# Turning the second attention's softmax weights of heads 0 to 3 on VectorE and by on-chip transfers

## The chip, the cores and the metric

The kernel runs on one core of a Trainium2 chip. A core has TensorE (PE, with its weight loads as PEld), VectorE (DVE), ScalarE (ACT), GpSimd (POOL) and SyncE (SP, which here only issues transfers). The metric is the device time of one launch in microseconds (us); before the change the median of 3 runs is 832.18 us (831.88 to 832.41).

## The reference

Two layers of a hybrid decoder on 256 tokens of width 1024 in float32. Each layer normalises the rows, multiplies by one wide matrix, and feeds three token mixers whose gated outputs are added; then comes a squared-ReLU MLP. The second attention ("MoBA") has 8 heads of width 64. Its block is 256 tokens long, as long as the sequence, so no earlier block can be selected and what is left is plain causal attention per head:

```python
s_own = jnp.einsum('bhqd,bhkd->bhqk', qc, k_own).astype(jnp.float32) * scale
s_own = jnp.where(kpos[None, :] <= qpos[:, None], s_own, NEG_INF)
p = jax.nn.softmax(jnp.concatenate([s_sel, s_own], axis=-1), axis=-1).astype(v.dtype)
o_own = jnp.einsum('bhqk,bhkd->bhqd', p[..., topk * BS:], v_own)
```

The scores leave TensorE with queries on the partitions, and so does the softmax. The product with the values sums over keys, and so needs the weights with keys on the partitions: the matrix p of every head has to be transposed ("turned").

## The kernel before

Every weight matrix is streamed from HBM in blocks of 128 by 1024 float32 (`raw`, seven buffers, issued by SP, L195). Each block is split into a rounded part by ScalarE (`whi`, L210) and a remainder by VectorE (`wlo`, L212), six buffers each, and a product is three matmuls over these parts (`three`, L231 to L233; for matrices kept transposed L412 and L414). A list of units, `prog`, holds the projections in order; `at(slot, step)` hangs smaller steps behind a unit, and a scheduler then orders each engine's instructions from this program order. What `tc.keep_in_program_order` or `tc.manual_schedule` covers stays where it was written. A transfer signals one of eight completion semaphores, taken in turn over all queues. A transfer that takes a semaphore again waits until the transfer that had it eight earlier has landed.

The second attention runs beside the projections around it. Its first slot is the second block of the gate projection `gmoba1`. The units behind it are two more blocks of `gmoba1`, four of the branch matrix `bmla`, four of `rqk` (queries and keys of the retention mixer), four of `rv`, four of `rg`, then the branch matrix `bmoba`, which is the first to read the attention's output.

- Scores (`together`, L481): heads 0 to 3 in the first slot, heads 4 to 7 eight slots later (`GAP = 8`). Each head's scores are one PSUM bank of three 128 by 128 squares: queries 0 to 127 with keys 0 to 127, then queries 128 to 255 with all 256 keys.
- Softmax (`attention_head`): VectorE adds the mask and finds maxima (L495, L498), ScalarE takes exponentials (L504), VectorE divides (L507, L509). The result is the tile `prob`, 128 by 384, four buffers.
- Turn (L512 to L518): three TensorE transposes into a PSUM bank `ps_pt` (L515) and one ScalarE copy into `probT` (L517). Heads 0 to 3 are turned three and four slots behind their scores, heads 4 to 7 likewise.
- Values (L542, L544): in `rg`, behind the retention scores (`ps_r`), eight heads at 64 columns, with `probT` as the moving operand. `split_plain` (L252) then writes `omobah` and `omobal`.

Around the change run the two rotary steps of the retention queries and keys (`rope_turned`, L439). For each pair of column blocks SP issues four on-chip transfers that swap groups of 32 partitions (`qkoth`, L434), GpSimd multiplies (L446), and VectorE adds (L449). The tile `gn`, the group norm's gains and offsets, is loaded behind the first block of `rqk` and used behind `rg`.

Of the kernel before, what the change touches and what calls it, by code (L numbers as in the profile page):

```python
# [7 lines left out]
F32 = mybir.dt.float32  # L8
F32R = mybir.dt.float32r
BF16 = mybir.dt.bfloat16  # L10
AF = mybir.ActivationFunctionType
# [3 lines left out]
P = 128  # L15
D = 1024
S = 256
# [120 lines left out]
def trunk(ctx: ExitStack, tc: tile.TileContext, gx, wts, consts, gfin, gn, xtok, out):  # L138


    nc = tc.nc
    _, where, _ = weight_plan()
# [3 lines left out]
    sb = ctx.enter_context(tc.tile_pool(name="sb", bufs=1))  # L146
# [71 lines left out]
    def acc_tile(name="acc"):  # L218
        return ps.tile([P, 512], F32, name=name, tag="acc", bufs=4)

    def misc_tile(name="misc"):
        return ps.tile([P, 512], F32, name=name, tag="misc", bufs=4)

    def w2k(name):
        return sb.tile([P, 512], F32, name=name, tag="w2k", bufs=W2K)

    def t4(name):
        return sb.tile([P, 4, S], F32R, name=name, tag="t4", bufs=T4)

# [11 lines left out]
    def small(name):  # L241
        return sb.tile([P, 8], F32, name=name, tag="st", bufs=SMALL)
# [8 lines left out]
    def split_plain(src, hi, lo):  # L251
        return nc.scalar.activation(hi, src, AF.Copy), nc.vector.tensor_sub(lo, src, hi.bitcast(F32))  # L252
# [212 lines left out]
    def in_a_row(*jobs):  # L465


        with tc.manual_schedule(engines={mybir.EngineType.PE}):
            rest = [job() for job in jobs]
        for job in rest:  # L470
            job()

    def together(parts, heads):

        for banks, a, b in heads:
            for o, sa, sb_ in parts:
                for j, bank in enumerate(banks):
                    rows = slice(64 * j, 64 * j + 64)  # L480
                    nc.tensor.matmul(bank[:, o], a[rows, sa], b[rows, sb_], start=True, stop=True)  # L481

    def attention_head(score, scale):


        got = {}

        def scores(s_ps=None):
            if s_ps is None:
                s_ps = misc_tile("ps_s")  # L490
                score(s_ps[:, 0:P], slice(0, P), slice(0, P))
                score(s_ps[:, P : 3 * P], slice(P, S), slice(0, S))
            p = sb.tile([P, 3 * P], F32, name="prob", bufs=4)
            m = small("smx")
            nc.vector.tensor_tensor_reduce(  # L495
                p[:, 0:P], s_ps[:, 0:P], mask[:, P : 2 * P], 1.0, NEG_INF, ALU.add, ALU.max, m[:, 0:1]
            )
            nc.vector.tensor_tensor_reduce(  # L498
                p[:, P : 3 * P], s_ps[:, P : 3 * P], mask, 1.0, NEG_INF, ALU.add, ALU.max, m[:, 1:2]
            )  # L500
            nc.vector.tensor_scalar(m[:, 2:4], m[:, 0:2], -scale, None, op0=ALU.mult)  # L501
            spans = ((0, P), (P, 3 * P))
            for i, (a, b) in enumerate(spans):
                nc.scalar.activation(  # L504
                    p[:, a:b], p[:, a:b], AF.Exp, bias=m[:, 2 + i : 3 + i], scale=scale, accum_out=m[:, 4 + i : 5 + i]
                )
            nc.vector.reciprocal(m[:, 6:8], m[:, 4:6])  # L507
            for i, (a, b) in enumerate(spans):
                nc.vector.tensor_scalar(p[:, a:b], p[:, a:b], m[:, 6 + i : 7 + i], None, op0=ALU.mult)  # L509
            got["p"] = p  # L510

        def turn():  # L512
            pt = misc_tile("ps_pt")
            for i, src in enumerate((0, P, 2 * P)):
                nc.tensor.transpose(pt[:, P * i : P * i + P], got["p"][:, src : src + P], ident)  # L515
            pT = sb.tile([P, 3 * P], F32, name="probT", bufs=8)
            nc.scalar.activation(pT, pt[:, : 3 * P], AF.Copy)  # L517
            return pT  # L518

        return scores, turn  # L520

    def attention(oT, score, vs, scale, first, group=None, former=None):

        pT = {}

        def turned(h, turn):
            pT[h] = turn()

        def values(h0):


            o, v = acc_tile("po"), vs()
            for h in (h0 + 2, h0):
                cs = slice(S * (h - h0) // 2, S * (h - h0) // 2 + S)
                for i in range(2):
                    for j in (1, 0):
                        vh = v[i][:, VD * (h + j) : VD * (h + j) + VD]
                        dst = o[64 * j : 64 * j + 64, cs]  # L540
                        if i == 0:
                            nc.tensor.matmul(dst, vh, pT[h + j][:, 0:S], start=True, stop=False)  # L542
                        else:
                            nc.tensor.matmul(dst[:, P:S], vh, pT[h + j][:, S : 3 * P], start=False, stop=True)  # L544
            dst = (part[:, h0 // 2 : h0 // 2 + 2, :].rearrange("p k s -> p (k s)") for part in oT)
            return lambda: split_plain(o, *dst)


        blocks = [lambda: values(4), lambda: values(0)]
        heads = [attention_head(lambda o, qs, ks, h=h: score(h, o, qs, ks), scale) for h in range(8)]  # L550
        if group is None:
            for h, (scores, turn) in enumerate(heads):
                at(first + h, scores)
                at(first + h + 2, lambda h=h, turn=turn: turned(h, turn))
            return blocks

        def four(h0):
            banks = group(h0)

            def rest():  # L560
                for h, bank in enumerate(banks, h0):
                    heads[h][0](bank)

            return rest


        at(first, lambda: in_a_row(*former, lambda: four(0)))
        at(first + GAP, lambda: in_a_row(lambda: four(4)))
        for i in range(2):
            for h in range(4):  # L570
                at(first + GAP * i + 3 + h // 2, lambda h=4 * i + h: turned(h, heads[h][1]))
        return blocks[::-1]

    def gates(l, key, xn):
# [44 lines left out]
    def begin(key, tag=None, bufs=None, queue=nc.sync, parts=None):  # L619
        if tag:  # L620
            started[key] = sb.tile([P, 512 if tag == "w2k" else 1024], F32, name="raw0", tag=tag, bufs=bufs)
        else:
            started[key] = wp.tile([P, 1024], F32, name="raw", bufs=RAW)
        transfer(key, started[key], queue, parts)


    c = slice(G_END - 2 * KD, G_END + S)
# [6 lines left out]
    xrows = [w2k("xrow") for _ in range(2 * NT)]  # L634
    begin((0, "b0mq", 1), "t4", T4, parts=((0, 416), (416, 928)))
    for k in range(2, KD):
# [5 lines left out]
        if k < 5:  # L642
            begin((0, "b0mq", k), "t4", T4, parts=((0, 416), (416, 928)) if k == 2 else None)
        else:
# [18 lines left out]
    def at(slot, step):  # L663
        steps.setdefault(slot, []).append(step)

    def slot(key, j):
        return [k for k, _ in prog].index((key, j))
# [9 lines left out]
    def layer(l, xn, before):  # L677

        c0 = []
        c, mla, mqkv, rqkv = {}, {}, {}, {}  # L680
# [216 lines left out]
        first = slot("mv", 3)  # L897
# [23 lines left out]
        first = slot("gmoba1", 1)  # L921
        at(first, lambda: omobaT.extend((t4("omobah"), t4("omobal"))))

        def moba_scores(h0):
            banks = [misc_tile("ps_s") for _ in range(4)][::-1]
            together(
                ((slice(0, P), slice(0, P), slice(0, P)), (slice(P, 3 * P), slice(P, S), slice(0, S))),
                [(banks[2 * i : 2 * i + 2], *(qkT[key][h0 // 4][:, i, :] for key in ("mq", "mk"))) for i in range(2)],
            )
            return banks  # L930

# [19 lines left out]
        def ret_scores():  # L951
            banks = [misc_tile("ps_r") for _ in range(RT_H)][::-1]
            together(
                ((slice(0, S), slice(0, P), slice(0, S)), (slice(S, 3 * P), slice(P, S), slice(P, S))),
                [(banks[2 * i : 2 * i + 2], rT[1][:, i, :], rT[0][:, i, :]) for i in (1, 0)],
            )

            def rest():
                for h in range(RT_H):
                    aT[h] = sb.tile([P, 3 * P], F32, name="retA", tag="prob", bufs=4)  # L960
                    nc.vector.tensor_mul(aT[h], banks[h][:, : 3 * P], rqkv["dec"][:, 384 * h : 384 * h + 384])

            return rest
# [67 lines left out]
            tc.keep_in_program_order(nc.sync.dma_start(rg["gn"], src))  # L1031

        project(l, "rg", xn, 512, rg_done)
        at(slot("rqk", 0), load_gn)
        branch(l, "bmoba", omobaT, th_moba, merged)
        th_ret = gates(l, "gret", xn)
        order_out = ExitStack()
# [207 lines left out]
        for t in range(NT):  # L1245
            y = sb.tile([P, D], F32, name="y", tag="t4", bufs=T4)
            r = sb.tile([P, 1], F32, name="fr", tag="st", bufs=SMALL)
# [39 lines left out]
FIRST = 4  # L1287
AHEAD = 1
GAP = 8
T4 = 8  # L1290
RAW = 7

# [79 lines left out]
```

## Time and profile before

| what | value |
|---|---|
| median of 3 runs | 832.18 us |
| profiled execution: time, span | 831.68 us, 829.9 us |
| PE busy, DVE busy, ACT busy, POOL busy | 823.1, 588.7, 484.4, 91.7 us |
| mean granted TensorE clock | 0.998 |
| transfers | 156.49 MB, mean 189 GB/s |

The span runs from the first to the last instruction; the run's own time is 1.8 us longer. A row of a timeline gives start, length, engine, line, operation and tiles, and "x6" merges six neighbours; matmuls are pipelined, so the length of one is not its cost: that is read from the difference between starts. In square brackets stands how long an engine was idle ahead of a row and what ended it. Times inside the span count from its start. The second attention of the first layer lies between some 108 and 160 us, that of the second layer between some 514 and 570 us.

### The profile page before, as it was taken

To read this page: it belongs to the slowest core of one execution; us is meant where nothing else is said; L and a number is where in the kernel's file an instruction comes from. 1 tells how busy PE (TensorE), PEld (TensorE's weight loads), DVE (VectorE), ACT (ScalarE), POOL (GpSimd) and SP (SyncE) were. 2 spreads that over 40 slices of the span, in tenths; PEclk is the share of its full clock that TensorE was granted. 3 is DMA by queue.
4 is the path that set the end of the run, shared out by engine and by line. 5 is a ranking of instruction groups with operands and counts; after the bars stand their busy time and mean duration, and the time that the engine had idled before them with its cause. 6 is when DMAs were issued, how large, how long until landed. Compare 5 with 4: busy or idle time off the path is not lost.

```text
span 829.9 us, 12157 instructions
## 1 busy us (share of the span) xinstructions
PE 823.1 (99%) x4363; PEld 700.6 (84%) x4363; DVE 588.7 (71%) x1059; ACT 484.4 (58%) x861; POOL 91.7 (11%) x75
## 2 busy tenths in 40 slices
PE   9999999999999999999999999999999999999997
PEld 7888878888888888888898887888888888888886
DVE  6877897595787566666697976677868766556663
ACT  7777666445556555555687575663545555555552
POOL 0100440030030000000036210012100300000000
PEclk9999999999999999999999999999999999999999
DMA  9966655546456666565557557564565665666611
GB/s 342 353 212 201 196 193 175 185 140 209 149 179 227 190 191 196 186 196 167 176 194 216 185 167 254 154 177 152 157 201 160 215 183 187 192 202 188 194 53 51
DMA packets 46524, 156.49 MB, mean 189 GB/s; under 512 B 5888, under 2 KB 7296, under 8 KB 46208
## 3 DMA queue, kind: packets, MB, share of 16 engines
q1 hardware_dynamic: 45888, 155.05, 58.5%
q8 instruction: 34, 0.56, 0.3%
q10 hardware_dynamic: 576, 0.67, 0.2%
q14 instruction: 26, 0.21, 0.1%
HBM read 150.98 MB, written 1.05 MB: 183 GB/s over the span
## 4 chain that ended last, share of the span: by engine, by line
PE 99%; DMA 0%; ACT 0%; DVE 0%; issue 0%; DVEq 0%
PE acc L231 18%; PE acc L232 18%; PE acc L233 18%; PE pup L1129 14%; PE pup L1131 7%; PE acc L1079 5%; PE acc L412 4%; PE acc L414 2%; PE ps_pt L515 1%; PE ps_s L901 1%; PE acc L746 1%; PE po L542 1%; PE ps_s L481 1%; PE acc L748 0%; PE po L544 0%; PE pmt L1045 0%
## 5 line engine op out<-in xcount | busy, mean ns | idle before, releaser
L212 DVE TENSOR_TENSOR wlo<-raw,whi 128x1024 fp32r<-128x1024 f32 (+4 forms) x287 | 346.5, 1214 | 179.2 <-ACT whi L210 120.1
L210 ACT ACTIVATE whi<-raw 128x1024 fp32r<-128x1024 f32 (+4 forms) x287 | 292.0, 1024 | 186.2 <-PE acc L233 94.9
L1129 PE MATMUL pup<-xs,whi 128*128 128x512 f32 x504 | 123.5, 390 | 0.0
L231 PE MATMUL acc<-whi,xs 128*128 128x512 f32 (+1 forms) x304 | 119.7, 395 | 0.0
L233 PE MATMUL acc<-whi,xs 128*128 128x512 f32 (+1 forms) x304 | 119.1, 392 | 0.0
L232 PE MATMUL acc<-wlo,xs 128*128 128x512 f32 (+1 forms) x304 | 118.8, 391 | 0.0
L1129 PEld LDWEIGHTS pup<-xs,whi 128*128 128x128 f32 x504 | 93.4, 188 | 18.6
L231 PE MATMUL acc<-whi,sq 128*128 128x512 f32 x256 | 100.1, 391 | 0.0
L232 PE MATMUL acc<-wlo,sq 128*128 128x512 f32 x256 | 99.9, 390 | 0.0
L233 PE MATMUL acc<-whi,sq 128*128 128x512 f32 x256 | 98.5, 389 | 0.0
L1131 PE MATMUL pup<-xs,wlo 128*128 128x256 f32 x504 | 69.6, 283 | 0.0
L1131 PEld LDWEIGHTS pup<-xs,wlo 128*128 128x128 f32 x504 | 66.6, 191 | 3.1
L231 PEld LDWEIGHTS acc<-whi,xs 128*128 128x128 f32 x304 | 57.1, 188 | 11.6 <-issue 1.0
L233 PEld LDWEIGHTS acc<-whi,xs 128*128 128x128 f32 x304 | 57.1, 188 | 11.3
L232 PEld LDWEIGHTS acc<-wlo,xs 128*128 128x128 f32 x304 | 57.2, 188 | 10.9
L233 PEld LDWEIGHTS acc<-whi,sq 128*128 128x128 f32 x256 | 48.0, 188 | 10.2
L1140 ACT ACTIVATE relu<-relu 128x256 f32<-128x256 f32 x64 | 25.5, 409 | 52.9 <-DVE relu L1139 52.9
L231 PEld LDWEIGHTS acc<-whi,sq 128*128 128x128 f32 x256 | 48.2, 188 | 9.2
L232 PEld LDWEIGHTS acc<-wlo,sq 128*128 128x128 f32 x256 | 48.2, 188 | 8.9
L288 POOL TENSOR_TENSOR sqsum<-sqsum,xsq 128x256 f32<-128x256 f32 x16 | 16.8, 1047 | 293.0 <-ACT xs L247 169.8
L504 ACT ACTIVATE prob<-prob,smx 128x128 f32<-128x128 f32 x64 | 28.4, 445 | 25.2 <-DVE smx L501 25.2
L412 PE MATMUL acc<-xs,whi 128*128 128x512 f32 x160 | 40.5, 395 | 0.0
(226 smaller groups left out, 1138.8 us busy)
## 6 DMA issues: line engine op xcount, KB each, us to landing
raw<-wts SPq DMA_DIRECT2D x264, 512.0 KB, 4.2
qkoth<-qkraw SPq DMA_DIRECT2D x48, 64.0 KB, 3.8
raw<-wts SPq DMA_DIRECT2D x5, 464.0 KB, 7.0
dec<-consts SPq DMA_DIRECT2D x2, 1024.0 KB, 6.4
raw<-wts SPq DMA_DIRECT2D x4, 416.0 KB, 3.2
raw<-wts SPq DMA_DIRECT2D x4, 256.0 KB, 4.1
xrow<-xtok SPq DMA_DIRECT2D x4, 256.0 KB, 7.4
gn<-gn SPq DMA_DIRECT2D x2, 512.0 KB, 8.4
```

The costliest lines, as they stand in the source:

```text
L210: nc.scalar.activation(hi[:, cs], raw[:, cs], AF.Copy)
L212: nc.vector.tensor_sub(lo[:, cs], raw[:, cs], hi[:, cs].bitcast(F32))
L231: nc.tensor.matmul(o, ah, bh, start=start, stop=False)
L232: nc.tensor.matmul(o, ah, bl, start=False, stop=False)
L233: nc.tensor.matmul(o, al, bh, start=False, stop=stop)
L288: (nc.gpsimd if n < self.on_pool else nc.vector).tensor_add(self.sum, self.sum, sq)
L412: nc.tensor.matmul(acc, wh[:, k, :], xn.both(k), start=k == 0, stop=False)
L504: nc.scalar.activation(p[:, a:b], p[:, a:b], AF.Exp, bias=m[:, 2 + i : 3 + i], scale=scale, accum_out=m[:, 4 + i : 5 + i])
L1079: nc.tensor.matmul(o, a, b, start=half == 0 and i == 0, stop=4 * half + n == KD and i == len(jobs) - 1)
L1129: nc.tensor.matmul(u, w, xm.both(k), start=k == 0, stop=False)
L1131: nc.tensor.matmul(u[:, 0:S], w, xm.k(k)[0], start=False, stop=k == KD - 1)
L1140: nc.scalar.activation(s, s, AF.Square)
```

## The change

Of the second attention's eight heads, 0 to 3 are turned in another way; heads 4 to 7 and the first attention stay on TensorE.

- VectorE transposes `prob` of a head in one instruction, in squares of 32 by 32: each square is turned, and stays within its 32 partitions. It writes into a tile `blocks` (128 by 1536, in the buffer of `KK`) where the 32-wide pieces of the four heads lie side by side.
- Sixteen on-chip transfers of 32 partitions by 384 elements (48 KB each) then move each group of squares from partition group a to b; they write `probT`, now one tile of 128 by 1536 for four heads. Eight are issued by SP and eight by ScalarE, in turn.
- The turns stand six and seven slots behind the scores (`TURN = 6`), the transfers behind the seventh, all kept in program order.
- TensorE reads the weights of heads 0 to 3 for the values in runs of 32 elements: a piece of 32 queries, then the next 384 elements further. The other four heads are read in one run as before.
- The first score matmul of heads 4 to 7 is kept in program order, and `gn`, which shares the `KK` buffer with `blocks`, is loaded four units later, behind the first block of `rv`.

```diff
-    def together(parts, heads):
+    def together(parts, heads, pinned=False):
...
-                    nc.tensor.matmul(bank[:, o], a[rows, sa], b[rows, sb_], start=True, stop=True)
+                    mm = nc.tensor.matmul(bank[:, o], a[rows, sa], b[rows, sb_], start=True, stop=True)
+                    if pinned:
+                        tc.keep_in_program_order(mm)
+                        pinned = False
...
-        def turn():
+        def turn(dst):
             pt = misc_tile("ps_pt")
...
-            pT = sb.tile([P, 3 * P], F32, name="probT", bufs=8)
-            nc.scalar.activation(pT, pt[:, : 3 * P], AF.Copy)
-            return pT
+            nc.scalar.activation(dst, pt[:, : 3 * P], AF.Copy)
+
+        def turn_blocks(dst):
+            return nc.vector.transpose(dst, got["p"])
...
+        def four_tile(h):
+            if h // 4 not in tiles:
+                tiles[h // 4] = sb.tile([P, 4 * 3 * P], F32, name="probT", bufs=2)
+            return tiles[h // 4]
...
+        def turned_blocks(h, turn):
+            if h == 0:
+                pT["blocks"] = sb.tile([P, 4 * 3 * P], F32, name="blocks", tag="KK", bufs=1)
+            by_head = (
+                z.rearrange("p (c t h j) -> p h t c j", c=4, t=3, h=4)[:, h] for z in (pT["blocks"], four_tile(h))
+            )
+            tc.keep_in_program_order(turn(next(by_head)))
+            o = next(by_head)
+            pT[h] = o[:, 0:2], o[:, 2]
+
+        def moved_blocks():
+            e = 3 * P
+            for a in range(4):
+                for b in range(4):
+                    src = pT["blocks"][32 * a : 32 * a + 32, e * b : e * b + e]
+                    queue = (nc.sync, nc.scalar)[b % 2]
+                    dma = queue.dma_start(four_tile(0)[32 * b : 32 * b + 32, e * a : e * a + e], src)
+                    tc.keep_in_program_order(dma)
...
-        for i in range(2):
-            for h in range(4):
-                at(first + GAP * i + 3 + h // 2, lambda h=4 * i + h: turned(h, heads[h][1]))
+        for h in range(4):
+            at(first + TURN + h // 2, lambda h=h: turned_blocks(h, heads[h][2]))
+            at(first + GAP + 3 + h // 2, lambda h=h + 4: turned(h, heads[h][1]))
+        at(first + TURN + 1, moved_blocks)
...
+                pinned=h0 > 0,
...
-        at(slot("rqk", 0), load_gn)
+        at(slot("rv", 0), load_gn)
...
+TURN = 6
```

More of the change, by code (lines that the diff above doesn't have):

```diff
@@ L515, in turn @@
                 nc.tensor.transpose(pt[:, P * i : P * i + P], got["p"][:, src : src + P], ident)
-            pT = sb.tile([P, 3 * P], F32, name="probT", bufs=8)
-            nc.scalar.activation(pT, pt[:, : 3 * P], AF.Copy)
-            return pT
-        return scores, turn
+            nc.scalar.activation(dst, pt[:, : 3 * P], AF.Copy)
+        def turn_blocks(dst):
+            return nc.vector.transpose(dst, got["p"])
+        return scores, turn, turn_blocks
     def attention(oT, score, vs, scale, first, group=None, former=None):
-        pT = {}
-        def turned(h, turn):
-            pT[h] = turn()
+        tiles, pT = {}, {}
+        def four_tile(h):
+            if h // 4 not in tiles:
+                tiles[h // 4] = sb.tile([P, 4 * 3 * P], F32, name="probT", bufs=2)
+            return tiles[h // 4]
+        def turned(h, turn):
+            o = four_tile(h)[:, 3 * P * (h % 4) : 3 * P * (h % 4) + 3 * P]
+            turn(o)
+            pT[h] = o[:, 0:S], o[:, S : 3 * P]
+        def turned_blocks(h, turn):
[15 more added lines that the diff above has]
+                    tc.keep_in_program_order(dma)
         def values(h0):
@@ L541, in values @@
                         if i == 0:
-                            nc.tensor.matmul(dst, vh, pT[h + j][:, 0:S], start=True, stop=False)
+                            nc.tensor.matmul(dst, vh, pT[h + j][0], start=True, stop=False)
                         else:
-                            nc.tensor.matmul(dst[:, P:S], vh, pT[h + j][:, S : 3 * P], start=False, stop=True)
+                            nc.tensor.matmul(dst[:, P:S], vh, pT[h + j][1], start=False, stop=True)
             dst = (part[:, h0 // 2 : h0 // 2 + 2, :].rearrange("p k s -> p (k s)") for part in oT)
@@ L551, in attention @@
         if group is None:
-            for h, (scores, turn) in enumerate(heads):
+            for h, (scores, turn, _) in enumerate(heads):
                 at(first + h, scores)
```

## The prediction

> **What bounds the kernel.** I read the page's busy times first, then the chain that ended last, then what TensorE waited for, and last the stretches that the change touches, engine by engine.
>
> ```profile
> PE 823.1 (99%) x4363; PEld 700.6 (84%) x4363; DVE 588.7 (71%) x1059; ACT 484.4 (58%) x861; POOL 91.7 (11%) x75
> PE acc L231 18%; PE acc L232 18%; PE acc L233 18%; PE pup L1129 14%; PE pup L1131 7%; PE acc L1079 5%; PE acc L412 4%; PE acc L414 2%; PE ps_pt L515 1%; PE ps_s L901 1%; PE acc L746 1%; PE po L542 1%; PE ps_s L481 1%; PE acc L748 0%; PE po L544 0%; PE pmt L1045 0%
> PE acc L746 <- ACT whi L210: 0.2, 1, 0.2
> ```
>
> PE is busy for 99% of the span, and the chain, in shares by line, is PE's from end to end. The third row is from PE's waits over the span (us, times, longest): it is the only wait of a matmul behind the start. So TensorE is fed all the time and its instruction stream sets the end. Whatever leaves that stream shortens the run by what it occupied, as long as TensorE stays fed; whatever the other engines gain or lose counts only where it makes TensorE wait. The turn itself (L515) is on the chain.
>
> **What leaves TensorE.** Per layer, three transposes for each of four heads. Their cost is read from starts, in PE's timeline, first layer and second:
>
> ```profile
> 116.04 0.93 PE L515 MATMUL ps_pt<-K,prob 128*128 128x128 f32 x6
> 116.72 0.48 PE L231 MATMUL acc<-whi,omlah 128*128 128x512 f32 x1
> 117.04 0.39 PE L232 MATMUL acc<-wlo,omlah 128*128 128x512 f32 x1
> 117.27 0.40 PE L233 MATMUL acc<-whi,omlal 128*128 128x512 f32 x1
> 117.51 0.39 PE L231 MATMUL acc<-whi,omlah 128*128 128x512 f32 x1
> 117.74 0.49 PE L515 MATMUL ps_pt<-K,prob 128*128 128x128 f32 x3
> 117.98 0.48 PE L232 MATMUL acc<-wlo,omlah 128*128 128x512 f32 x1
> 118.30 0.49 PE L515 MATMUL ps_pt<-K,prob 128*128 128x128 f32 x3
> 118.55 0.48 PE L233 MATMUL acc<-whi,omlal 128*128 128x512 f32 x1
> 118.86 0.39 PE L231 MATMUL acc<-whi,omlah 128*128 128x512 f32 x1
> ```
> ```profile
> 523.87 0.82 PE L515 MATMUL ps_pt<-K,prob 128*128 128x128 f32 x6
> 524.45 0.48 PE L231 MATMUL acc<-whi,omlah 128*128 128x512 f32 x1
> 524.76 0.39 PE L232 MATMUL acc<-wlo,omlah 128*128 128x512 f32 x1
> ...
> 527.29 0.82 PE L515 MATMUL ps_pt<-K,prob 128*128 128x128 f32 x6
> 527.87 0.47 PE L231 MATMUL acc<-whi,omlah 128*128 128x512 f32 x1
> 528.18 0.39 PE L232 MATMUL acc<-wlo,omlah 128*128 128x512 f32 x1
> ```
>
> A plain 512-wide matmul takes 0.23 us from start to start (117.04 to 117.27). From 116.04 to 118.86 are 2.82 us with twelve transposes and six such matmuls: 2.82 - 6 x 0.23 = 1.44 us. In the second layer each group of six stands with one matmul: 0.89 - 0.23 = 0.66, twice, 1.32 us. Both layers: 2.76 us leave the stream, 0.115 us a transpose.
>
> **What TensorE may pay back: the strided reads.** Here is PE's timeline of the values of all eight heads.
>
> ```profile
> 155.90 0.65 PE L542 MATMUL po<-probT,mv 128*64 128x256 f32 x4
> 157.25 0.60 PE L542 MATMUL po<-probT,mv 128*64 128x256 f32 x4
> 158.65 0.50 PE L231 MATMUL acc<-whi,xs 128*128 128x512 f32 x1
> ```
>
> Four heads take 157.25 - 155.90 = 1.35 us. Heads 0 to 3 now read runs of 32 elements. No row of before has such an operand, so the bounds are nothing (the count of elements is the same) and a doubling, 1.35 us a layer. I take nothing: 32 in a row is near to the contiguous case, not to single elements. The Trainium skill, "Advanced Engine Details and Errata", section Memory Cachelines, says that SBUF is read in lines of 16 bytes and that repeated hits on a line keep the full rate; by that a run of 128 bytes costs nothing. The same section, under PSUM, has the sentence "Any non-contiguous AP significantly slows down matmuls"; taken literally it speaks against the change and gives the second rival. No row here shows either.
>
> **ScalarE and VectorE.** ScalarE loses four copies a layer (L517) and gains eight issues; VectorE gains four transposes. The nearest rows are these, of ACT, of DVE, and one of PE.
>
> ```profile
> 129.42 0.35 ACT L394 COPY second<-acc 128x256 f32<-128x256 f32 x1
> 133.49 0.40 ACT L504 ACTIVATE prob<-prob,smx 128x128 f32<-128x128 f32 x1 [3.71 <-DVE smx L501]
> 134.38 1.05 ACT L210 ACTIVATE whi<-raw 128x1024 fp32r<-128x1024 f32 x1
> 137.97 0.34 ACT L394 COPY second<-acc 128x256 f32<-128x256 f32 x1
> ```
> ```profile
> 126.81 1.22 DVE L212 TENSOR_TENSOR wlo<-raw,whi 128x1024 fp32r<-128x1024 f32 x1 [0.58 <-ACT whi L210]
> 127.95 0.41 DVE L394 TENSOR_TENSOR qkraw<-acc,second 128x256 f32<-128x256 f32 x1
> 135.46 1.22 DVE L212 TENSOR_TENSOR wlo<-raw,whi 128x1024 fp32r<-128x1024 f32 x1 [0.20 <-ACT whi L210]
> 156.73 1.94 DVE L961 TENSOR_TENSOR retA<-ps_r,dec 128x384 f32<-128x384 f32 x4
> ```
> ```profile
> 136.52 0.40 PE L231 MATMUL acc<-whi,xs 128*128 128x512 f32 x1
> 149.08 0.39 PE L232 MATMUL acc<-wlo,xs 128*128 128x512 f32 x1
> ```
>
> A VectorE transpose of 384 columns I price at 0.49 us, a quarter of the L961 row, which has the same 384 columns; ends 0.41 (the L394 row, 256 columns) and 1.22 (the 1024-wide row). Four are 2 us a layer, with idle time beside them. The remainder made at 135.46 (the first block of `rg`) is first read by TensorE at 149.08: 12.4 us in hand, so the 2 us are hidden.
>
> **The transfers.** Rows of SP, then the tile of the swaps (two groups of four) with its GpSimd and VectorE steps.
>
> ```profile
> 128.06 3.07 SPq L195 DMA_DIRECT2D raw<-wts  x2
> 131.22 3.91 SPq L434 DMA_DIRECT2D qkoth<-qkraw  x4
> ```
> ```profile
> L434 SPq DMA_DIRECT2D qkoth<-qkraw x8: 512/584/2082, 131.2 to 145.1; - x8
> L446 POOL TENSOR_TENSOR qkoth<-qkoth,tab x1: 1294/1294/1294, 137.7 to 137.7; 128x512 f32<-128x512 f32 x1
> L449 DVE TENSOR_TENSOR qkT<-qkT,qkoth x1: 693/693/693, 139.0 to 139.0; 128x512 f32<-128x512 f32 x1
> DMA to landing us min/median/max: 2.7/3.8/5.8
> ```
> ```profile
> raw<-wts SPq DMA_DIRECT2D x264, 512.0 KB, 4.2
> gn<-gn SPq DMA_DIRECT2D x2, 512.0 KB, 8.4
> ```
>
> A swap of the same kind and size occupies its queue for 0.58 us and lands after 3.8. I follow the first layer on the clock of before, 1.4 us earlier, since TensorE, which paces all, has by then lost its twelve transposes. In the changed instruction order ScalarE's issues stand behind the second `second` copy (ends 129.77) and ahead of the exponentials of heads 4 to 7; VectorE's last transposes behind the add at 127.95. So the train starts at about 128.4. Eight semaphores serve the sixteen, so each queue's last four wait for landings of the first: ScalarE's fourth waits for the weight block issued just ahead, when the split of 126.81 has ended (128.03 - 1.4 = 126.6, landed at 130.8), its eighth for that fourth (130.8 + 3.8 = 134.6, behind the seventh); ScalarE is free at about 135.5 (133.0 without any such wait; 145 if all eight took the longest, 2.08).
>
> Behind ScalarE's issues wait the exponentials: 137.97 - 133.49 less the split of 1.05 = 3.4 us, done at 138.9, divided at some 139.7. TensorE's first transpose of heads 4 to 7 stands 41 matmuls into `rv`: 136.52 - 1.4 + 41 x 0.23 = 144.5. In hand: 4.8 us. The splits that follow the exponentials on ScalarE had the 12 us shown and keep some 6.
>
> Behind SP's eight wait the first pair's swaps. The last of these takes the semaphore of ScalarE's sixth, which waited for its second (129.0 + 3.8 = 132.8) and lands at 136.6; so the swap lands at 140.4, GpSimd makes it 141.7, VectorE's add 142.4. That add now stands ahead of the splits of `rg` on VectorE, with one multiply of about 0.7 between: the first is done at 142.4 + 0.7 + 1.2 = 144.3 and read at 149.08 - 1.4 = 147.7. In hand: 3.4 us, the smallest cover of all. If it is gone, each further us costs one us a layer. `gn` waits for all sixteen, is issued near 139.5, lands within 8.4 and is needed by `rg`'s multiplies past 160. The weight block behind it lands before 150; ScalarE splits it after that. The pinned score matmul changes no place on TensorE. The second layer has the same order.
>
> **The sum.** 831.68 (the profiled execution) - 2.76 = 828.9; that execution lies 0.5 below the median, so 829.4 on the median's scale.
>
> **Rivals.** *Slower: the train of transfers is late.* The first rope add holds VectorE ahead of `rg`'s splits, and three landings in series lead to it. At the longest landing above, 5.8 for 3.8, it is 6.0 us late, 2.6 past the cover, in both layers: 832.2 - 2.8 + 5.2 = 834.6. It turns slower than 0.2% where the three together are 5.6 us late (3.4 of cover, 1.4 of gain, 0.8). For it: one swap was issued in 2.08 us, and transfers of two queues at once are not in the trace. Against: that row stood behind a 512 KB weight block. *Strided reads double the values:* 2.7 us back, 832.2, no change. Against it only the length of the runs. *A shorter wait eats half:* ScalarE or the rope add is late by 0.7 us past its cover in each layer: 830.8, also within what can't be told from no change. For it: the cover of 3.4 us is built of estimates.
>
> **How the numbers follow.** A measurement of this kernel can tell about 0.2%, 1.7 us. The forecast, all of it hidden, 829.4, has 0.68, since TensorE's own saving is read off rows and each cover is over 3 us; late train 0.12; strided reads 0.08; half eaten 0.12, of which 0.02 still falls under 830.5. So faster 0.70, no difference 0.18, slower 0.12. The forecast's own range is 828.8 to 830.2; the range takes in both cases of no change, up to 832.4, and leaves out the late train.
>
> **What would show it.** Right: 24 transposes fewer in the turn's line, PE busy near 820, no new wait of PE; the values of four heads still 1.35 us; ScalarE's eight issues ended before 137 on the clock of before; the first rope add done 3 us ahead of the split that TensorE reads. Wrong: a gap in PE ahead of `rg`'s first block or of heads 4 to 7's transposes, transfers taking 5.5 us or more to land, or values at twice their time.

## The result

The changed kernel takes 829.18 us (828.62 to 829.56, 6 runs) against 832.12 us (831.8 to 832.8, 6 runs) of the kernel before on the same chip: a ratio of 0.9964, with a 95% interval of 0.9951 to 0.9977. That is 2.9 us, or 0.36%, faster. Its profiled execution takes 829.56 us with a span of 827.8 us.

These are PE's busy time and the chain's shares by line, from the page of the changed kernel, and the one row of PE's waits over its span.

```profile
PE 821.3 (99%) x4339; PEld 699.1 (84%) x4339; DVE 592.6 (72%) x1067; ACT 480.2 (58%) x853; POOL 97.7 (12%) x75
PE acc L231 18%; PE acc L233 18%; PE acc L232 18%; PE pup L1166 14%; PE pup L1168 7%; PE acc L1116 5%; PE acc L412 4%; PE acc L414 2%; PE ps_s L937 1%; PE acc L782 1%; PE ps_pt L518 1%; PE po L577 1%; PE ps_s L481 1%; PE warm L693 0%; PE ac
PE warm L693 <- PEq L1404: 0.8, 1, 0.8
```

There are 24 instructions fewer on PE, the chain is still TensorE's, and no matmul behind the start waits for another engine. How much left the stream is read from matmuls that both kernels have: one ahead of the first layer's turns, one behind its values, and one behind the values of the second layer. PE's timeline of before, then of after:

```profile
115.80 0.40 PE L233 MATMUL acc<-whi,omlal 128*128 128x512 f32 x1
162.20 0.39 PE L231 MATMUL acc<-whi,xs 128*128 128x512 f32 x1
571.30 0.39 PE L231 MATMUL acc<-whi,xs 128*128 128x512 f32 x1
```
```profile
116.80 0.39 PE L233 MATMUL acc<-whi,omlal 128*128 128x512 f32 x1
161.62 0.40 PE L231 MATMUL acc<-whi,xs 128*128 128x512 f32 x1
569.24 0.39 PE L231 MATMUL acc<-whi,xs 128*128 128x512 f32 x1
```

The first stands 1.00 us later, the second 0.58 earlier, the third 2.06 earlier. So layer one gives 1.58 us and layer two 1.48, 3.06 in all, against 2.76 in the prediction. The 1.00 us comes from the start of this execution, long before the first changed instruction. 0.85 of it is seen in the first four matmuls and their follower, before and after:

```profile
4.59 1.17 PE L746 MATMUL acc<-xs,whi 128*128 128x512 f32 x4 [0.20 <-ACT whi L210]
5.59 0.34 PE L754 MATMUL b<-whi,xs 128*128 128x416 f32 x1
```
```profile
4.57 2.05 PE L782 MATMUL acc<-xs,whi 128*128 128x512 f32 x4
6.42 0.43 PE L790 MATMUL b<-whi,xs 128*128 128x416 f32 x1
```

Before, four matmuls took 1.00 us from start to start (4.59 to 5.59), after 1.85 (4.57 to 6.42). It is not a mark of the change: in the version below that turns all eight heads this way, the first of the three matmuls stands at 115.74. That is why the two spans differ by 2.1 us only; the medians differ by 2.9, close to what the stream lost.

The parts of the change, in the changed kernel: the rows of the tile `blocks` (lengths in ns, least, median and most; the last row is in us), and PE's values of the first four heads, which read runs of 32.

```profile
L563 ACTq DMA_DIRECT2D probT<-blocks x16: 514/604/1350, 130.2 to 544.7; - x16
L563 SPq DMA_DIRECT2D probT<-blocks x16: 507/585/1252, 130.2 to 544.4; - x16
L523 DVE STREAM_TRANSPOSE blocks<-prob x8: 530/550/570, 125.6 to 536.5; 128x384 f32<-128x384 f32 x8
DMA to landing us min/median/max: 1.9/2.7/4.6
```
```profile
158.53 0.65 PE L577 MATMUL po<-probT,mv 128*64 128x256 f32 x4
159.88 0.60 PE L577 MATMUL po<-probT,mv 128*64 128x256 f32 x4
```

Four heads take 159.88 - 158.53 = 1.35 us, to the hundredth what they took before.

What came near to costing time is the way to the first split of `rg` on VectorE. Rows of ACT, DVE, GpSimd and PE in the first layer, in this order:

```profile
130.18 7.29 ACTq L563 DMA_DIRECT2D probT<-blocks  x8
137.51 0.40 ACT L507 ACTIVATE prob<-prob,smx 128x128 f32<-128x128 f32 x1 [8.24 <-DMA probT<-blocks]
```
```profile
129.13 1.02 DVE L523 STREAM_TRANSPOSE blocks<-prob 128x384 f32<-128x384 f32 x2
138.53 0.17 DVE L510 RECIPROCAL smx<-smx 128x2 f32<-128x2 f32 x1 [3.83 <-ACT prob L507]
141.37 1.50 DVE L512 TENSOR_SCALAR prob<-prob,smx 128x128 f32<-128x128 f32 x2
143.45 0.68 DVE L449 TENSOR_TENSOR qkT<-qkT,qkoth 128x512 f32<-128x512 f32 x1
144.65 5.75 DVE L212 TENSOR_TENSOR wlo<-raw,whi 128x1024 fp32r<-128x1024 f32 x5
```
```profile
141.22 1.30 POOL L446 TENSOR_TENSOR qkoth<-qkoth,tab 128x512 f32<-128x512 f32 x1 [25.66 <-DMA qkoth<-qkraw]
```
```profile
148.29 0.62 PE L231 MATMUL acc<-whi,xs 128*128 128x512 f32 x2
148.75 0.40 PE L232 MATMUL acc<-wlo,xs 128*128 128x512 f32 x1
```

ScalarE issues for 7.3 us; only then come the exponentials of heads 4 to 7, and VectorE sits idle for 3.83 us for them (the bracket at 138.53). From there on it is busy: divisions, the rope add, then the splits from 144.65. One of the five takes about 1.15 us (5.75 / 5), so the first is done at 145.8, and TensorE reads it at 148.75. In hand are 2.9 us. The rope add does not set this: GpSimd had its operand ready at 141.22 + 1.30 = 142.52, and VectorE came to it at 143.45.

### The profile page after: what moved, and what is told of

The parts are those of the page before. It is cut to its first block, busy times and chain, and to the rows that moved or that the text cites. A ratio compares the mean times of both kernels' runs of the same rounds, so it can differ in the third digit from the quotient of the medians.

```text
span 827.8 us, 12148 instructions
## 1 busy us (share of the span) xinstructions
PE 821.3 (99%) x4339; PEld 699.1 (84%) x4339; DVE 592.6 (72%) x1067; ACT 480.2 (58%) x853; POOL 97.7 (12%) x75
## 4 chain that ended last, share of the span: by engine, by line
PE 99%; DVE 0%; ACT 0%; issue 0%; DVEq 0%
PE acc L231 18%; PE acc L233 18%; PE acc L232 18%; PE pup L1166 14%; PE pup L1168 7%; PE acc L1116 5%; PE acc L412 4%; PE acc L414 2%; PE ps_s L937 1%; PE acc L782 1%; PE ps_pt L518 1%; PE po L577 1%; PE ps_s L481 1%; PE warm L693 0%; PE acc L784 0%; PE pmt L1082 0%
## 5 line engine op out<-in xcount | busy, mean ns | idle before, releaser
L232 PE MATMUL acc<-wlo,xs 128*128 128x512 f32 (+1 forms) x304 | 118.9, 391 | 0.0
L231 PE MATMUL acc<-whi,xs 128*128 128x512 f32 (+1 forms) x304 | 118.6, 394 | 0.0
L231 PE MATMUL acc<-whi,sq 128*128 128x512 f32 x256 | 100.1, 391 | 0.0
L232 PE MATMUL acc<-wlo,sq 128*128 128x512 f32 x256 | 99.9, 390 | 0.0
L231 PEld LDWEIGHTS acc<-whi,xs 128*128 128x128 f32 x304 | 57.1, 188 | 11.3 <-issue 0.7
L232 PEld LDWEIGHTS acc<-wlo,xs 128*128 128x128 f32 x304 | 57.1, 188 | 10.9
L231 PEld LDWEIGHTS acc<-whi,sq 128*128 128x128 f32 x256 | 48.2, 188 | 9.2
L232 PEld LDWEIGHTS acc<-wlo,sq 128*128 128x128 f32 x256 | 48.2, 188 | 8.9
L446 POOL TENSOR_TENSOR qkoth<-qkoth,tab 128x512 f32<-128x512 f32 x12 | 23.3, 1944 | 161.1 <-DMA qkoth<-qkraw 161.1
```

What stands on the lines that cost most here:

```text
L231: nc.tensor.matmul(o, ah, bh, start=start, stop=False)
L232: nc.tensor.matmul(o, ah, bl, start=False, stop=False)
L446: mul = on.tensor_mul(*operands)
```

## The experiments

The forecast says that TensorE's stream alone decides, with everything else hidden. The rivals say that the gain comes from something else (the moved order), that strided reads cost, or that the train of transfers is nearly late. Four kernels were run beside one set of runs of before (median 831.87 us), and four more beside another (831.81 us).

### The turn back on TensorE, all else left as changed

```diff
-            at(first + TURN + h // 2, lambda h=h: turned_blocks(h, heads[h][2]))
+            at(first + TURN + h // 2, lambda h=h: turned(h, heads[h][1]))
...
-        at(first + TURN + 1, moved_blocks)
```

> The changed kernel with its later turn, the wider tile, the pinned score and the later load of gn, but heads 0 to 3 turned on TensorE as before; no transfers. Theory (the gain is the 24 transposes and nothing else): the gain is gone, 831.7 to 832.6, and the turn's line has 96 transposes. Rival (the gain comes from the new order): it stays below 830.5.

Measured: 831.77 us (831.39 to 832.26), ratio 0.9998, interval 0.9989 to 1.0007. The whole gain is gone when the 24 transposes return, so neither the later slots, nor the pinned score matmul, nor the later `gn` brought any of it that could be measured. The same three matmuls as above, in this run:

```profile
115.75 0.39 PE L233 MATMUL acc<-whi,omlal 128*128 128x512 f32 x1
162.00 0.39 PE L231 MATMUL acc<-whi,xs 128*128 128x512 f32 x1
571.00 0.39 PE L231 MATMUL acc<-whi,xs 128*128 128x512 f32 x1
```

From the first to the second are 46.25 us here and 161.62 - 116.80 = 44.82 in the changed kernel: 1.43 us for the twelve transposes of layer one. From the second to the third are 409.00 and 407.62: 1.38 for those of layer two. Together 2.81.

### The layout alone, runs of 32

Heads 0 to 3 are turned on TensorE as before the change, and ScalarE writes them into the changed layout.

```diff
+            if group is not None and h < 4:
+                v = four_tile(h).rearrange("p (c t h j) -> p h t c j", c=4, t=3, h=4)[:, h]
+                turn(v)
+                pT[h] = v[:, 0:2], v[:, 2]
+                return
```

> Heads 0 to 3 turned on TensorE at the old slots; only the layout is the changed one, so that the values read runs of 32 elements. Theory (runs of 32 are free): 831.7 to 832.6, the values of four heads 1.35 us from start to start. Rival (any broken run costs TensorE): up to 1.35 us more in each layer, up to 835.

Measured: 832.11 us (831.51 to 832.44), ratio 1.0, interval 0.9991 to 1.0009: no change, as the theory said.

### The layout alone, single elements

The same, with the four heads interleaved element by element, so that TensorE reads one element in every 16 bytes.

```diff
+                v = four_tile(h).rearrange("p (q h) -> p h q", h=4)[:, h]
+                turn(v)
+                pT[h] = v[:, 0:S], v[:, S : 3 * P]
```

> As the one before, in the same instruction order, but the four heads' weights are interleaved element by element, so that the values read every fourth element, 16 bytes apart. If only the count of elements sets TensorE's read: 1.35 us for four heads and about 832.2. If a run has to fill a line of 16 bytes: the values of four heads take longer, at twice the time 2.7 us and about 835.

Measured: 835.17 us (834.24 to 835.21), ratio 1.0035, interval 1.0022 to 1.0047. These are the starts of the first values of heads 0 to 3 and the start of what follows them, in PE's timeline, with runs of 32, then with single elements:

```profile
156.55 0.65 PE L582 MATMUL po<-probT,mv 128*64 128x256 f32 x4
157.90 0.60 PE L582 MATMUL po<-probT,mv 128*64 128x256 f32 x4
```
```profile
156.65 1.10 PE L582 MATMUL po<-probT,mv 128*64 128x256 f32 x4
159.38 0.62 PE L582 MATMUL po<-probT,mv 128*64 128x256 f32 x4
```

157.90 - 156.55 = 1.35 us, as without any stride; 159.38 - 156.65 = 2.73, twice that. So a doubling exists, and the rival had its price right (1.38 us in this layer, 2.8 in two; the run lost 3.1 against the one with runs of 32 and 3.3 against before); but it belongs to single elements, and a run of 32 is free. The Trainium skill, "Advanced Engine Details and Errata", section Memory Cachelines, asks for repeated hits on a 16-byte line of SBUF for full rate, and both runs agree with it: 1.35 us with every element of a line used, 2.73 with one. Its sentence that any non-contiguous pattern significantly slows matmuls stands under PSUM there, and the run of 32 shows that it doesn't hold for every operand in SBUF.

### All eight heads by VectorE and transfers

Heads 4 to 7 take the same way, with a second train; `gn`, whose buffer serves the second `blocks`, is loaded behind the first block of `rg`.

```diff
-            at(first + GAP + 3 + h // 2, lambda h=h + 4: turned(h, heads[h][1]))
-        at(first + TURN + 1, moved_blocks)
+            at(first + GAP + T2 + h // 2, lambda h=h + 4: turned_blocks(h, heads[h][2]))
+        at(first + TURN + 1, lambda: moved_blocks(0))
+        at(first + GAP + T2 + 1, lambda: moved_blocks(4))
...
-        at(slot("rv", 0), load_gn)
+        at(slot("rg", 0), load_gn)
...
+T2 = 4
```

> Heads 4 to 7 turned in the same way as well, by a second train of sixteen transfers, gn loaded behind the first block of rg. Theory (the price of a turn on TensorE is all that counts, as long as it is covered): twice the gain, 826.5. Rival (the second train holds ScalarE and SP until the values or the splits of rg are late): a wait of TensorE in each layer, no faster than 829.2, up to 833.

Measured: 828.33 us (827.88 to 829.19), ratio 0.9956, interval 0.9944 to 0.9969. That is only a little below the changed kernel, and between the theory (826.5) and the rival (829.2 or more). A new wait explains a part. PE's waits, and rows of VectorE and of GpSimd around it in the second layer:

```profile
PE acc L233 <- DVE omobal L252: 1.3, 1, 1.3
```
```profile
568.38 4.54 DVE L212 TENSOR_TENSOR wlo<-raw,whi 128x1024 fp32r<-128x1024 f32 x2
572.84 1.28 DVE L252 TENSOR_TENSOR omobal<-po,omobah 128x512 fp32r<-128x512 f32 x2
```
```profile
568.35 1.27 POOL L1062 TENSOR_TENSOR rgb<-rg,gn 128x512 f32<-128x512 f32 x1 [13.12 <-DMA gn<-gn]
569.70 2.13 POOL L1063 TENSOR_TENSOR rg<-rg,gn 128x512 f32<-128x512 f32 x1
```

The remainder of the attention's output stands on VectorE behind two weight splits. They take 4.54 us, where five in a row took 1.15 each in the changed kernel, and `bmoba` waits 1.3 us for the remainder. Beside them GpSimd multiplies by `gn`, released by the landing of `gn` that this version delays. GpSimd's second multiply ends at 569.70 + 2.13 = 571.83, and the second split 1.09 us later, at 572.92, about what one split takes alone. So the stretch fits a collision of the two engines (last section), and what it adds, 4.54 - 2 x 1.15 = 2.2 us, is more than the wait. No run has this order on VectorE without GpSimd beside it, so the collision is the likely cause and not a shown one.

### The train twice

The sixteen transfers are issued a second time, behind the first.

```diff
-            for a in range(4):
-                for b in range(4):
+            for a, b in 2 * [(a, b) for a in range(4) for b in range(4)]:
```

> The sixteen transfers are issued twice, the second pass behind the first, with the same sources and destinations; nothing else is edited. The order of the instructions behind them is made anew, with the same 72 transposes of TensorE. Each queue is held by eight further issues (8 x 0.58 = 4.6 us, and waits for landings), so everything behind the train comes 5 to 8 us later. Theory (the train costs nothing as long as it fits in its covers, the smallest of which came out at some 2.7 us): the covers are now too short; if the order stays, TensorE waits 2 to 5 us in each layer, ahead of the first block of rg, and the time is 833 to 839 us; where the new order moves what waits, less, but over 830. Rival (the transfers have far more room than the covers say, since everything is made blocks ahead): 829.2 within 0.5.

Measured: 835.16 us (834.33 to 836.69), ratio 1.0039, interval 1.0027 to 1.0052: slower than before the change, and within the 833 to 839 expected. PE's waits, then the splits of `rg` on DVE and their readers on PE in the first layer:

```profile
PE acc L232 <- DVE wlo L212: 3.5, 2, 1.8
```
```profile
149.17 3.48 DVE L212 TENSOR_TENSOR wlo<-raw,whi 128x1024 fp32r<-128x1024 f32 x3
```
```profile
147.86 0.74 PE L231 MATMUL acc<-whi,xs 128*128 128x512 f32 x2
150.44 0.50 PE L232 MATMUL acc<-wlo,xs 128*128 128x512 f32 x1 [1.84 <-DVE wlo L212]
```

TensorE waits once in each layer, at the first split of `rg`, where the smallest cover was said to lie. The size can be checked. The clocks of two executions differ, so the first L231 of `rg` serves as zero. In the changed kernel the splits begin 148.29 - 144.65 = 3.64 us ahead of it, here 149.17 - 147.86 = 1.31 behind: 4.95 later. From that L231 to the L232 it is 0.46 us in the changed kernel (148.29 to 148.75) and 2.58 here: 2.12 lost. So 4.95 - 2.12 = 2.83 us were in hand, against the 2.9 read off directly. Put shorter, the read follows the start of the splits by 4.10 us there and by 1.27 here, where TensorE waits for it.

### The train on one queue

All sixteen are issued by SyncE, or all by ScalarE.

```diff
-                    queue = (nc.sync, nc.scalar)[b % 2]
+                    queue = nc.sync
```

> All sixteen transfers are issued by SyncE. ScalarE is free 7.3 us earlier in each layer, SyncE is held for 16 x 0.58 = 9.3 us and more by waits for landings, so the swaps of the queries' rope and the weight blocks behind them come some 4 us later. Theory (TensorE's stream decides, ScalarE's eight issues were hidden): no gain from freeing ScalarE; 829.2 within 0.7 if the rope add keeps its cover, up to 832 if the 4 us exceed its 2.7. Rival (ScalarE's 7.3 us were what half of the gain was lost to): under 828.5.

Measured: 828.99 us (828.67 to 829.62), ratio 0.9964, interval 0.995 to 0.9978. Freeing ScalarE gains nothing, and no matmul waits, so ScalarE's 7.3 us in the changed kernel were hidden.

```diff
-                    queue = (nc.sync, nc.scalar)[b % 2]
+                    queue = nc.scalar
```

> All sixteen transfers are issued by ScalarE. SyncE's swaps and weight blocks come 4.7 us earlier, ScalarE is held for 9.3 us and more, some 12 with its waits, in each layer, so the exponentials of heads 4 to 7 and the splits behind them come 4 to 5 us later. Theory: their cover was 4.2 to 6 us, so the time is 829.2 within 0.7, or up to 2 us more where a part of the cover is missing. Rival (SyncE's hold delays the weight stream and costs something already): under 828.5.

Measured: 830.97 us (830.23 to 831.92), ratio 0.9988, interval 0.9979 to 0.9997. Some 2.1 of the 2.9 us are gone. TensorE waits twice for that split, once in each layer. Rows of ACT, DVE and PE in the first layer:

```profile
129.51 13.27 ACTq L563 DMA_DIRECT2D probT<-blocks  x16
```
```profile
140.98 0.69 DVE L449 TENSOR_TENSOR qkT<-qkT,qkoth 128x512 f32<-128x512 f32 x1 [6.95 <-POOL qkoth L446]
143.85 0.17 DVE L510 RECIPROCAL smx<-smx 128x2 f32<-128x2 f32 x1 [2.17 <-ACT prob L507]
148.55 4.62 DVE L212 TENSOR_TENSOR wlo<-raw,whi 128x1024 fp32r<-128x1024 f32 x4
```
```profile
148.00 0.72 PE L231 MATMUL acc<-whi,xs 128*128 128x512 f32 x2 [0.21 <-ACT whi L210]
149.82 0.50 PE L232 MATMUL acc<-wlo,xs 128*128 128x512 f32 x1 [1.11 <-DVE wlo L212]
```

This run parts the two chains that could hold VectorE. SyncE is free, so the rope add comes early (140.98), and yet the same split is late: VectorE waits for the exponentials (143.85), which wait for ScalarE's 13.27 us of issues. By the same reckoning the splits begin 0.55 us behind the first L231 (148.55 - 148.00), 4.19 later than in the changed kernel, and 1.82 - 0.46 = 1.36 us are lost: again 2.83 in hand.

### All eight heads, the second train on SyncE alone

```diff
-                    queue = (nc.sync, nc.scalar)[b % 2]
+                    queue = (nc.sync, nc.scalar)[b % 2] if h0 == 0 else nc.sync
```

> As e4 (all eight heads turned by VectorE and by two trains), but the second train is issued by SyncE alone. In e4 TensorE waited 1.3 us in the second layer for the remainder of the attention's output, which VectorE made behind two splits of weights that had come late. With ScalarE free of the second train the splits come earlier. Theory: that wait goes or shrinks, 827.0 to 828.3. Rival: the second train holds SyncE for 9.3 us and delays the weight blocks further, 828.5 or more.

Measured: 827.08 us (826.57 to 827.13), ratio 0.9939, interval 0.9926 to 0.9951: faster than both kernels. PE has 48 instructions fewer than before (4315). The one row of its waits, and the second layer's second split on DVE and first multiply by `gn` on GpSimd:

```profile
PE warm L694 <- PEq L1406: 0.8, 1, 0.8
```
```profile
569.47 1.22 DVE L212 TENSOR_TENSOR wlo<-raw,whi 128x1024 fp32r<-128x1024 f32 x1
570.75 1.27 POOL L1062 TENSOR_TENSOR rgb<-rg,gn 128x512 f32<-128x512 f32 x1 [15.99 <-DVE wlo L212]
```

The wait that the version with both queues had is gone, and the time is the one expected, but not clearly for the reason expected. The splits start only a little earlier (567.72, where it was 568.38); the plainer difference is that they take 1.2 us each. `gn` stands on SyncE behind the longer train, lands at 570.6 and not at 568.2, and GpSimd begins at 570.75, when both splits are done. The first half of the remainder also stands between the two splits here, no longer behind both. Which of these removed the wait was not separated.

This version gains 4.7 us over before. Forty-eight transposes at the prediction's 0.115 us would be 5.5. The remaining 0.8 was not taken apart.

## Why the prediction was right

The forecast was 829.4 us, within 828.8 to 830.2; measured were 829.18.

**What leaves TensorE.** The mechanism held, and so did the term: 24 transposes were put at 2.76 us, and when they return, they cost 1.43 + 1.38 = 2.81. Between before and after the stream lost 3.06. The other 0.25 us lies between before and the run with the turn back on TensorE, which have equally many instructions in a different order (46.40 and 46.25 us, 409.10 and 409.00). It was not forecast, and it was not taken apart. PE is busy for 821.3 us, "near 820", with no new wait.

**Strided reads.** The value taken, nothing, was right (1.35 us), and the upper bound was a real price for another stride (2.73).

**VectorE's transposes** were priced at 0.49 us and take 0.55, within the ends given. **The issues** take 0.585 and 0.604 for the 0.58 assumed. **The landings** were put at 3.8 and have a median of 2.7. In the first layer, transfer by transfer, the first seven, issued right behind a 512 KB block of weights, take 4.05 to 4.52 us, and the nine behind them 1.87 to 2.10. `gn` lands in 4.1 rather than up to 8.4.

**ScalarE.** On the prediction's clock the execution after lies 0.8 us later (1.4 us earlier than before was assumed; 0.58 was it). ScalarE was forecast free at 135.5 + 0.8 = 136.3 and is at 137.5. The train began at 130.2 and not at 129.2, because VectorE's last two transposes ended only then (129.13 + 1.02), but that is not what held ScalarE. Its first three issues are over at 132.3, and the next waits until 134.26. SP's weight block and ScalarE's last five issues in the changed kernel:

```profile
128.90 0.33 SPq L195 DMA_DIRECT2D raw<-wts  x1
```
```profile
134.26 3.21 ACTq L563 DMA_DIRECT2D probT<-blocks  x5
```

The fourth issue waits for the weight block, as the prediction had it, but that block landed at 134.2 (5.3 us after its issue) and not at 130.8 + 0.8 = 131.6. The eighth was to wait once more, for a landing of 3.8 us; the landings now take 2.0, and the five issues follow each other. One error makes it 2.6 us later, the other takes back over half of that, so that 136.3 came near to 137.5 is in part luck. The criterion "ended before 137 on the clock of before" can be read in two ways: on the shifted clock of the prediction's sum the end is 137.5 - 0.8 = 136.7 and meets it, on the clock of before unshifted it is 138.1 and misses it by 1.1 us. The cover took it.

**The smallest cover** was put at the right place, the first split of `rg` on VectorE, and near its size: 3.4 forecast, 2.9 read, 2.83 from each of two runs that overdrew it. But the step that leads there was wrong, and the nearness of the size is luck. The prediction had it held by the rope add, behind SyncE's swaps and three landings in series, and gave ScalarE's chain another cover, 4.8 us up to the transposes of heads 4 to 7. In truth the divisions of heads 4 to 7 stand ahead of that same split in VectorE's queue, so ScalarE's train, the exponentials and the divisions run into it, and this chain is the one that ends last. What the prediction left out is this order on VectorE: it followed the exponentials to their next reader on TensorE and not to what is queued behind the divisions. The rope path itself met its time, 141.7 + 0.8 = 142.5 forecast for GpSimd's end and 142.52 measured, but not by three landings in series: SP waited once, until 134.63, for the train's first landings, its issues then followed each other up to the last swap, issued at 139.08, and that one landed in 2.0 us. Errors of opposite sign met there. The add ended at 143.45 + 0.68 = 144.13, 4.6 us ahead of TensorE's read, so that sign came true.

**The rivals.** Late train: the mechanism is real and did not occur; the doubled train makes it occur, and the kernel is then 0.39% slower than before. The prediction set the point of turning at 5.6 us late. The run was 4.95 us late in the first layer and well past that point already: the cover is 2.83 and not 3.4 us, and the first wait had a cost behind it (last section). Half eaten: this is what the train on ScalarE alone does, and more: some 2.1 us of the gain go where that rival had 1.4, with a loss of 1.36 us in the first layer where 0.7 had been assumed in each. (Its 830.8 lies near the 830.97 in part because before ran 0.4 us faster beside this run.) Strided reads: this rival falls. One reading in the rivals was wrong without consequence: transfers of two queues at once do stand in the trace of before, where ScalarE and SyncE both issue loads at 0.74 us and at 1.18.

## What to carry to other kernels

Where TensorE's stream sets the end, count what leaves it and then look for the one instruction of another engine that TensorE reads next behind the moved work; the room there is the budget for everything that is added, and an engine's queue has to be followed past the instruction one has in mind to all that stands behind it. A train of transfers costs its issuing queue half a microsecond each and more where a semaphore comes round, so it belongs on the queue whose followers have the most time: the same sixteen cost nothing on SyncE and 2 us on ScalarE. A layout that keeps runs of 32 elements costs TensorE nothing, one that takes single elements out of 16 bytes doubles its reads.

## What the runs showed of the hardware

- A short wait of TensorE can cost more than itself. Behind the wait of 1.84 us in the run with the doubled train the granted clock fell. This is PE in two stretches of that run, ahead of and behind its first L232 (columns: stretch, length, PE busy, granted clock, share of the transfer engines, GB/s):

```profile
148.00:150.40 2.40, 0.60 (x2) 1.00 0.57 200
151.70:155.10 3.40, 3.40 (x10) 0.51 0.99 329
```

In PE's timeline two matmuls of this stretch, nine starts apart:

```profile
151.70 0.54 PE L232 MATMUL acc<-wlo,xs 128*128 128x512 f32 x1
155.34 0.40 PE L232 MATMUL acc<-wlo,xs 128*128 128x512 f32 x1
```

The nine took 3.64 us where the pace of 0.23 needs 2.1, so 1.6 us were lost on top of the wait. The transfer engines were busier there too (0.99 for 0.57); a granted clock of about half is by itself enough to cost this. Behind the wait of 1.70 us in the second layer of the same run, and behind that of 1.11 in the run with the train on ScalarE, the clock stayed at 1.00, so the length of the wait alone doesn't decide it; what does stays open.
- Two of VectorE's divisions that take 0.55 us elsewhere took 1.50 beside GpSimd's multiply (141.37 on VectorE, 141.22 to 142.52 on GpSimd, both shown above). In the doubled train it is the same, 1.48, and where GpSimd's multiply ran earlier, with the train on ScalarE, the last two divisions took 0.55. The Trainium skill, "Trainium Architecture — The Big Picture", section What this means for kernel authors, calls the port that the two engines share an exclusive lock; these three traces agree with that.
